# A two-layer transformer block on one core: the last low part of each group of seven products made by ScalarE and an accumulating DMA instead of VectorE

## The chip, the cores and the metric

The kernel runs on one core of one Trainium2 chip. The metric is the device time of one launch in microseconds (us), the median of several runs; lower is better. The core's engines have their own queues and run side by side: TensorE (PE in the profile; PEld is its weight load), VectorE (DVE), ScalarE (ACT), GpSimd (POOL) and SyncE (SP). PE, DVE and ACT compute; SP only issues DMAs here, and POOL issues DMAs and does some elementwise work.

## The reference, cut to what matters

Two layers of the same block are applied to 528 tokens of width 1024 (16 meta tokens and 512 inputs), all in fp32:

```python
def hybrid_layer(x, norm_g, w_in, ...):
    h = rms_norm(x, norm_g)
    q, k, v, gate_a, u_b, gate_b, q_idx, k_idx, w_idx, merge = split(h @ w_in)
    ...                                   # norms and rotary embedding on q, k, q_idx, k_idx
    attn = indexer_sparse_attention(...)  # scores by an indexer, the best 128 keys, softmax, values
    y_a = (attn * silu(gate_a)) @ w_a
    pooled = multiscale_pool(u_b, ...)
    y_b = (pooled * silu(gate_b)) @ w_b
    g_a, g_b = split(sigmoid(merge))
    return x + (g_a * y_a + g_b * y_b) @ w_out
```

What the change touches is how the products with `gate_a` and `merge` (512 + 2048 columns of `w_in`) and with half of `w_out` are computed, in both layers.

## The kernel before

**Split operands.** Each fp32 operand X of a large matmul is held as two tiles of the PE's faster fp32r format: a high part, X rounded, and a low part, X minus that rounded copy. A product is then three matmuls: high by high, high by low, low by high. For weights, ScalarE makes the high part (a copy that rounds) and, in most places, VectorE the low part (a subtraction). For some chunks of weights (`by_dma`) the low part is made another way: ScalarE writes the negated rounded copy, and a DMA that adds (`accum_op=OP.add`, issued by POOL) puts the fp32 weights on top of it, `minus` in L222 to L226.

**Chunks.** Weights come from memory in chunks of 1024 by 256, two raw tiles each, loaded by SP (`w_fetch`), with room for two chunks (four raw tiles). A raw tile is overwritten by the load of the chunk after next once its last reader is done. High and low parts go to a ring of eight `w` tiles of 128 partitions by 1024 elements.

**Groups of seven products.** The chunks in `mixed` (twelve per layer, 24 in all: ten for `gate_a` and `merge`, two for `w_out`) are multiplied by the Strassen-Winograd scheme: weights and activations are cut into 2 by 2 blocks, and seven block products take the place of eight. Each needs a block or a sum of blocks of the weights, called `a12`, `a11`, `s2`, `s1`, `s3`, `s4`, `a22` in the code, each with a high and a low part in one `w` tile. `group_of_products` (L1068) issues the products in the order a11, a12, s2, s1, s3, s4, a22. A product is twelve matmuls: for each of four slices of the depth, (high, high), (high, low), (low, high), weights first. So the low part of a block is first needed by the third matmul of its product. All products of a group add up in three PSUM banks; ScalarE copies partial sums out after a11 (`p1`), s2 (`u2`) and s1 (`p5`), and a product that adds on top of a bank must wait for the copy of it.

**Order of the work.** The preparation of a chunk is a list of nine items, i0 to i8 (`mixed_prep`, L262). Items are taken from a queue as the products go: by the end of product d of a group, at least items up to 5 + 9d/7 of that group have been issued (`LEAD` is 5). So i6 is issued after the second product, i7 after the third and i8 after the fourth. The program order is the queue order for PE and DVE (`manual_schedule`). For ACT, POOL and SP a scheduler orders the instructions when the kernel is built, with an own estimate of times; `marked()` keeps an ACT instruction behind the latest copy out of PSUM that was noted in `mark[0]`, here the copy `p1` for i6 and `u2` for i7.

The items that matter here: i5 makes the high part of s3; i6 the low part of s3, the high part of s4, and issues `first_sum(c + 1)` (L260, an accumulating DMA that adds two blocks of the next chunk); i7 makes the low part of s4 and the high part of a22; i8 the low part of a22, after which the raw tiles are free and `w_load` issues the load of the chunk after next. i1 issues the DMA of L289, which adds s2 onto a12 to give s4.

Between the products, the steps of attention (transposes, logits, values) are issued to PE as filling (`pump`), and the steps that pick the best keys on DVE (MAX8 and MATCH_REPLACE8) are issued as long as a running balance `spare` of estimated PE time minus estimated DVE time is positive (`group_done`, L379). A low part counts 0.60 us in it (`dve_cost`).

Of the kernel before, what the change touches and what calls it, by code (L numbers as in the profile page):

```python
# [10 lines left out]
AF = mybir.ActivationFunctionType  # L11
OP = mybir.AluOpType
# [79 lines left out]
def tile_block(ctx: ExitStack, tc: tile.TileContext, x, meta, w_in, pool_w, w_a, w_b, w_out, rows, hgain, c_tab, out):  # L92
    nc = tc.nc
    act, gp = nc.scalar, nc.gpsimd
# [8 lines left out]
    def f(ap):  # L103
        return ap.bitcast(F32)
# [54 lines left out]
    def w_load():  # L159
        if W["load"] < len(chunks):  # L160
            c = w_place()
            for s in range(2):
                w_fetch(c, s)
# [10 lines left out]
    def w_tile():  # L174
        return wpool.tile([128, 1024], F32R, tag="w", name="w", bufs=8)

    def w_prep_enqueue(casts_first=False, after=None):
# [9 lines left out]
        if c in mixed:  # L187
            prep_q.extend(mixed_prep(c))
            return
# [64 lines left out]
    def marked():  # L254

        return tc.issue_after(mark[0]) if mark[0] else nullcontext()

    def first_sum(c):
        if c in mixed:
            gp.dma_start(raws[c][0][:, 1], raws[c][0][:, 0], accum_op=OP.add)  # L260

    def mixed_prep(c):  # L262

        r0, r1 = raws[c]
        blk = {"a11": r0[:, 0], "a21": r0[:, 1], "a12": r1[:, 0], "a22": r1[:, 1]}
        src = {"a11": "a11", "a12": "a12", "a22": "a22", "s3": "a21", "s2": "s2", "s1": "a11", "s4": "a12"}
        ops = ready[c]
        soon = c <= len(chunks) - 2

        def hi(n):  # L270
            t = w_tile().rearrange("p (s k e) -> p s k e", s=2, k=4)
            ops[n] = t
            with marked():
                act.copy(t[:, 0], blk[src[n]])  # L274

        def lo(n):
            dve.tensor_sub(ops[n][:, 1], blk[src[n]], f(ops[n][:, 0]))

        def i0():
            hi("a12")  # L280
            if soon:
                hi("a11")

        def i1():
            lo("a12")
            blk["s2"] = tmp.tile([128, 544], F32, tag="L", name="s2", bufs=LB)[:, :512].rearrange(
                "p (k e) -> p k e", k=4)
            dve.tensor_add(blk["s2"], blk["a21"], blk["a22"])
            gp.dma_start(blk["a12"], blk["s2"], accum_op=OP.add)  # L289
            (lo if soon else hi)("a11")  # L290

        def i2():
            if not soon:
                lo("a11")
            dve.tensor_sub(blk["a11"], blk["s2"], blk["a11"])

        def i3():
            hi("s2")

        def i4():  # L300
            lo("s2")
            hi("s1")

        def i5():
            lo("s1")
            hi("s3")

        def i6():
            lo("s3")
            hi("s4")  # L310
            first_sum(c + 1)

        def i7():
            lo("s4")
            hi("a22")

        def i8():
            lo("a22")
            del raws[c]
            w_load()  # L320

        def counted(fn):
            def item():
                fn()
                progress[c] += 1
            return item

        progress[c] = 0
        return [counted(fn) for fn in (i0, i1, i2, i3, i4, i5, i6, i7, i8)]

    def flush_prep():
# [1377 lines left out]
```

## Time and profile before

| | |
|---|---|
| median of 3 runs | 728.59 us (727.71 to 729.0) |
| profiled execution | span 726.5 us from the first to the last instruction; no other time of it is given |
| instructions | 16015 |
| DVE busy | 613.6 us (84%) |
| ACT busy | 505.0 us (70%) |
| POOL busy | 256.2 us (35%) |
| mean granted TensorE clock | 0.999 |

The 24 groups lie in four stretches of the span: ten from 167 to 304 us and two from 345 to 367 us (first layer), ten from 521 to 655 us and two from 698 to 720 us (second layer). From one group to the next pass 10.9 to 19.5 us, the longer ones with much filling.

How to read it: a row of the grouped views gives the line, engine, operation, output and inputs, shapes, count, then the busy time in us and the mean of one in ns, then the idle time of the engine just before them and what ended it. All PE and DVE instructions have line 63 (the helper that counts their time); they are told apart by their tiles. `w<-raw,w` on DVE is a low part, `w<-raw` on ACT at L274 a high part, `d<-...` on PE a product into a bank. A row of the timeline gives the start, the duration and how many instructions were merged. PE's busy share says little by itself, since matmuls overlap.

### The profile page before, as it was taken

To read this page: it belongs to the slowest core of one execution; us is meant where nothing else is said; L and a number is where in the kernel's file an instruction comes from. 1 tells how busy PE (TensorE), PEld (TensorE's weight loads), DVE (VectorE), ACT (ScalarE), POOL (GpSimd) and SP (SyncE) were. 2 spreads that over 40 slices of the span, in tenths; PEclk is the share of its full clock that TensorE was granted. 3 is DMA by queue.
4 is the path that set the end of the run, shared out by engine and by line. 5 is a ranking of instruction groups with operands and counts; after the bars stand their busy time and mean duration, and the time that the engine had idled before them with its cause. 6 is when DMAs were issued, how large, how long until landed. Compare 5 with 4: busy or idle time off the path is not lost.

```text
span 726.5 us, 16015 instructions
## 1 busy us (share of the span) xinstructions
PE 720.1 (99%) x5829; PEld 693.9 (96%) x5829; DVE 613.6 (84%) x1546; ACT 505.0 (70%) x1162; POOL 256.2 (35%) x347
## 2 busy tenths in 40 slices
PE   9999999999999999999999999999999999999998
PEld 8999998899999999999999989998899999999997
DVE  5887999998998875888968779999989987768774
ACT  7679735686788887656545796367789888875643
POOL 3751174631222211062447411867041231106200
PEclk9999999999999999999999999999999999999999
DMA  8767765874564434677551788677464554448932
GB/s 268 236 162 176 169 150 117 220 162 100 127 136 117 97 79 117 175 225 182 147 165 59 182 186 197 162 168 164 105 160 103 135 127 93 113 114 268 199 93 73
DMA packets 107406, 109.49 MB, mean 151 GB/s; under 512 B 5888, under 2 KB 86448, under 8 KB 107328
## 3 DMA queue, kind: packets, MB, share of 16 engines
q1 hardware_dynamic: 94576, 74.84, 34.3%
q0 software_dynamic: 12672, 33.56, 25.9%
q8 instruction: 46, 0.75, 0.4%
q14 instruction: 32, 0.26, 0.1%
q10 hardware_dynamic: 80, 0.08, 0.0%
HBM read 66.35 MB, written 8.55 MB: 103 GB/s over the span
## 4 chain that ended last, share of the span: by engine, by line
PE 83%; DVE 7%; DMA 4%; ACT 2%; issue 2%; POOL 1%; SPq 0%; DVEq 0%; ACTq 0%; POOLq 0%
PE d L63 67%; PE a L63 11%; PE v L63 4%; DVE w L63 2%; DMA wo<-raw 1%; DMA w<-raw 1%; DMA xt<-in_x_dram 1%; DMA kept<-res 1%; DMA res<-kept 1%; DVE lt L63 1%; DVE sc L63 1%; POOL hlo L1527 1%; DVE c L63 0%; DVE zb L63 0%; DMA raw<-in_w_out_dram 0%
## 5 line engine op out<-in xcount | busy, mean ns | idle before, releaser
L63 PE MATMUL d<-hhi,w 128*128 128x256 f32 (+3 forms) x1248 | 252.9, 292 | 0.4 <-DVE c L63 0.3
L63 PEld LDWEIGHTS d<-hhi,w 128*128 128x128 f32 x1248 | 200.1, 188 | 4.2 <-DVE c L63 0.7
L63 PE MATMUL d<-hlo,w 128*128 128x256 f32 (+3 forms) x624 | 172.6, 289 | 0.0
L63 DVE TENSOR_TENSOR w<-raw,w 128x512 fp32r<-128x512 f32 (+1 forms) x160 | 119.6, 755 | 13.3 <-ACT w L274 13.1
L63 PEld LDWEIGHTS d<-hlo,w 128*128 128x128 f32 x624 | 117.8, 189 | 1.4 <-issue 0.2
L63 PE MATMUL d<-hsum,w 128*128 128x264 f32 (+1 forms) x720 | 95.1, 285 | 0.0
L274 ACT CAST w<-raw 128x512 fp32r<-128x512 f32 x144 | 86.0, 623 | 9.2 <-DMA raw<-s 4.7
L63 PEld LDWEIGHTS d<-hsum,w 128*128 128x128 f32 x720 | 89.7, 188 | 1.0 <-issue 0.5
L63 PE MATMUL d<-w,hhi 128*128 128x256 f32 x576 | 85.9, 287 | 0.0
L63 PEld LDWEIGHTS d<-w,hhi 128*128 128x128 f32 x576 | 74.7, 188 | 4.5 <-issue 2.7
L260 POOL DMA_DIRECT2D raw<-raw x24 | 21.6, 899 | 131.0 <-DMA raw<-in_w_in_dram 21.1
L63 DVE MATCH_REPLACE8 sc<-m,sc 128x400 f32<-128x400 f32 (+2 forms) x100 | 54.4, 548 | 0.0
L63 DVE MAX8 m<-sc 128x8 f32<-128x400 f32 (+2 forms) x100 | 53.4, 557 | 0.9
L226 POOL DMA_DIRECT2D w<-raw x36 | 32.6, 929 | 61.1 <-ACT w L225 44.5
L289 POOL DMA_DIRECT2D raw<-s x24 | 21.2, 885 | 77.7 <-DVE s L63 28.1
L852 ACT ACTIVATE lt<-lt,mn,NR 128x144 f32<-128x144 f32 (+3 forms) x64 | 42.2, 662 | 8.2 <-DVE mn L63 8.0
L63 PE MATMUL d<-mhi,w 128*128 128x272 f32 (+2 forms) x192 | 45.7, 325 | 0.2 <-ACT sq L701 0.2
L63 PE MATMUL d<-w,hlo 128*128 128x256 f32 x288 | 45.6, 281 | 0.0
L867 POOL TENSOR_SCALAR pm<-lt,rs 128x16 f32<-128x16 f32 x48 | 27.9, 604 | 45.8 <-DVE rs L63 42.0
L773 ACT ACTIVATE r<-a,wab 128x272 f32<-128x272 f32 (+2 forms) x80 | 35.4, 489 | 8.2 <-PE a L63 7.9
L225 ACT ACTIVATE w<-raw 128x1024 fp32r<-128x1024 f32 x36 | 37.5, 1057 | 4.3 <-PE d L63 4.3
L1527 POOL TENSOR_TENSOR hlo<-ta,hhi 128x256 fp32r<-128x256 f32 (+1 forms) x28 | 24.9, 898 | 40.5 <-PE d L63 28.9
(270 smaller groups left out, 1642.1 us busy)
## 6 DMA issues: line engine op xcount, KB each, us to landing
raw<-in_w_in_dram SPq DMA_DIRECT2D x88, 256.0 KB, 3.3
w<-raw POOLq DMA_DIRECT2D x36, 512.0 KB, 5.9
raw<-in_w_in_dram SPq DMA_DIRECT2D x32, 512.0 KB, 4.4
raw<-raw POOLq DMA_DIRECT2D x24, 256.0 KB, 4.0
raw<-s POOLq DMA_DIRECT2D x24, 256.0 KB, 3.3
kept<-res SPq DMA_DIRECT2D x16, 264.0 KB, 3.5
res<-kept SPq DMA_DIRECT2D x16, 264.0 KB, 5.5
raw<-in_w_branch_b_dram SPq DMA_DIRECT2D x8, 512.0 KB, 4.6
```

The costliest lines, as they stand in the source:

```text
L63: return fn(*a, **k)
L225: act.activation(t, raws[c][s], AF.Copy, scale=-1.0)
L226: gp.dma_start(t, raws[c][s], accum_op=OP.add)
L260: gp.dma_start(raws[c][0][:, 1], raws[c][0][:, 0], accum_op=OP.add)
L274: act.copy(t[:, 0], blk[src[n]])
L289: gp.dma_start(blk["a12"], blk["s2"], accum_op=OP.add)
L773: act.activation(r[:, n - 1::-1] if i == 0 else r[:, o:o + e], ps[:, :e], AF.Relu, scale=wab[:, i, h:h + 1])
L852: act.activation(L[hh][:, :n], L[hh][:, :n], AF.Exp, scale=NR[:, i, h:h + 1], bias=mn[:, hh:hh + 1], accum_out=sm[:, hh:hh + 1])
L867: (gp if j < 3 else dve).tensor_scalar(pms[i][:, 2 * j + hh, :], L[hh][:, 0:16], rs[:, hh:hh + 1], None, op0=OP.mult)
L1527: pool_end = gp.tensor_sub(hlo[:, j, a:a + n], d, f(hhi[:, j, a:a + n]))
```

## The change

In i6 the high part of a22 is made right after that of s4, and its low part follows at once by a new helper: ScalarE writes the negated rounded copy into the low half of the tile, and a DMA issued by POOL adds the fp32 block. The low part of a22 on DVE (in i8) is gone; `first_sum(c + 1)` moves from i6 to i7. Nothing else differs. This happens in each of the 24 groups.

```diff
+        def far_lo(n):
+            with marked():
+                act.activation(ops[n][:, 1], blk[src[n]], AF.Copy, scale=-1.0)
+            gp.dma_start(ops[n][:, 1], blk[src[n]], accum_op=OP.add)
...
         def i6():
             lo("s3")
             hi("s4")
-            first_sum(c + 1)
+            hi("a22")
+            far_lo("a22")
 
         def i7():
             lo("s4")
-            hi("a22")
+            first_sum(c + 1)
 
         def i8():
-            lo("a22")
             del raws[c]
             w_load()
```

## The prediction, made before the change was run

> **What bounds the kernel now.** I read the page first (busy shares, the chain that ended last), then PE's waits, then four stretches that hold the 24 groups of seven products, then single groups in the timeline.
>
> ```profile
> span 726.5 us, 16015 instructions
> PE 720.1 (99%) x5829; PEld 693.9 (96%) x5829; DVE 613.6 (84%) x1546; ACT 505.0 (70%) x1162; POOL 256.2 (35%) x347
> PE 83%; DVE 7%; DMA 4%; ACT 2%; issue 2%; POOL 1%; SPq 0%; DVEq 0%; ACTq 0%; POOLq 0%
> ```
>
> PE is never idle for long: 726.5 - 720.1 = 6.4 us in the whole span. Busy time can hide small stalls, because matmuls overlap; so the waits of the weight load (PEld) are the better witness. All of those that name DVE's low parts, DVE's sums or ACT's copies out of PSUM:
>
> ```profile
> PEld d L63 <- ACT p L1095: 1.0, 2, 0.7
> PEld d L63 <- DVE w L63: 1.0, 4, 0.3
> PEld d L63 <- DVE c L63: 0.7, 2, 0.5
> ```
>
> (us in total, times, longest.) That is 2.7 us in all, 0.37% of the span. The four stretches, with columns PE, PEld, DVE, ACT and POOL busy, clock, DMA share and GB/s:
>
> ```profile
> 165.00:305.00 140.00, 139.67 (x1212) 136.37 (x1211) 117.28 (x317) 112.31 (x273) 27.71 (x41) 1.00 0.48 114
> 343.00:368.00 25.00, 24.43 (x196) 23.82 (x195) 23.54 (x37) 13.72 (x29) 11.79 (x15) 1.00 0.64 168
> 520.00:655.00 135.00, 134.68 (x1197) 131.97 (x1196) 113.32 (x308) 111.36 (x268) 28.73 (x41) 1.00 0.50 117
> 696.00:722.00 26.00, 25.81 (x216) 25.36 (x216) 17.47 (x37) 12.60 (x31) 0.86 (x1) 1.00 0.24 61
> ```
>
> In the ten-group stretches DVE (84%) and ACT (80 to 82%) are nearly equally full, and PE has no idle time to speak of. So the change moves work between two engines that both lie beside PE. It can pay only by ending waits of PE, and cost only by making new ones.
>
> **The change, part by part.**
>
> *DVE loses 24 low parts.*
>
> ```profile
> L63 DVE TENSOR_TENSOR w<-raw,w 128x512 fp32r<-128x512 f32 x144 | 99.3, 696 | 13.3 <-ACT w L274 13.1
> L274 ACT CAST w<-raw 128x512 fp32r<-128x512 f32 x144 | 86.0, 623 | 9.2 <-DMA raw<-s 4.7 <-DVE raw L63 2.9 <-DMA raw<-in_w_out_dram 1.1
> L225 ACT ACTIVATE w<-raw 128x1024 fp32r<-128x1024 f32 x36 | 37.5, 1057 | 4.3 <-PE d L63 4.3
> L230 ACT CAST w<-raw 128x1024 fp32r<-128x1024 f32 x36 | 37.3, 1051 | 0.0
> ```
>
> 24 x 0.696 = 16.7 us of DVE. None of it lies on PE's path except where PE waited for DVE. Moreover the pacing in `group_done` counts 0.60 us for a low part and gives what is not used to the selection steps: while these last, the freed time is filled at once. The gain is therefore between 0 and the 2.7 us above. The waits for other low parts and for the sums that stand behind them in DVE's queue can end in part; I take 0.8, about half of the two DVE rows (1.7).
>
> *ACT gains 24 negated copies.* A scaled copy of 1024 elements costs what a cast costs (1057 against 1051 ns), so one of 512 costs what the cast of 512 does, 0.62 us: 24 x 0.62 = 14.9 us. In the ten-group stretches ACT goes from 112.3 to 118.5 of 140 us, 85%. Queued behind the two copies that now come after `hi("s4")` are `u2` and `p5`; the product that adds onto the same bank waits for each. The waits in between take up part of the shift (below, 0.71 us in the second group). Bounds for what PE loses: 0, and 1.0 (the two late copies of the ACT row above, once more). I take 0.4, nearer to 0, since 22 of 24 groups have no such wait now.
>
> *POOL gains 24 accumulating DMAs of 256 KB.*
>
> ```profile
> L260 POOL DMA_DIRECT2D raw<-raw x24 | 21.6, 899 | 131.0 <-DMA raw<-in_w_in_dram 21.1 <-DVE mn L63 19.9 <-DMA raw<-in_w_out_dram 19.3
> L289 POOL DMA_DIRECT2D raw<-s x24 | 21.2, 885 | 77.7 <-DVE s L63 28.1 <-issue 15.3 <-DVE c L63 13.4
> DMA to landing us min/median/max: 3.2/3.3/4.6
> DMA to landing us min/median/max: 3.3/4.0/5.3
> ```
>
> The last two rows are L289's and L260's: from the start of the issue to the landing. Both are DMAs of the new one's kind and size, 0.9 us of POOL each; 24 x 0.9 = 21.6 us on an engine 35% busy. L289 mostly runs alone; L260 starts while loads of raw tiles are in flight. The new one starts then too (below), so I take 4.0, with 3.2 and 5.3 as ends.
>
> The Trainium skill, page DMA: Bandwidth & Descriptors, section Anatomy of one DMA, gives about 2.0 us plus the bytes over 436 GB/s for a DMA issued by GpSimd. That would be 2.6 us for 256 KB, an estimate by that page; no row here goes below 3.2, so the measurement decides, and by the page alone no group below would be late.
>
> *The critical term: does a22's low part arrive in time?* Now it takes 0.69 us of DVE behind the high part. Then it takes a second ACT copy, a POOL issue and a landing. In the second group (rows of ACT, DVE, PE, POOL and SP's queue):
>
> ```profile
> 180.93 1.15 ACT L274 CAST w<-raw 128x512 fp32r<-128x512 f32 x2
> 182.79 0.69 ACT L866 ACTIVATE lt<-lt,rs 128x128 f32<-128x128 f32 x2 [0.71 <-DVE rs L63]
> 183.97 0.61 ACT L274 CAST w<-raw 128x512 fp32r<-128x512 f32 x1
> 184.61 0.69 DVE L63 TENSOR_TENSOR w<-raw,w 128x512 fp32r<-128x512 f32 x1
> 187.70 0.41 PE L63 MATMUL d<-hhi,w 128*128 128x264 f32 x2
> 182.86 0.91 POOL L867 TENSOR_SCALAR pm<-lt,rs 128x16 f32<-128x16 f32 x2 [3.81 <-DVE rs L63]
> 182.31 3.94 SPq L154 DMA_DIRECT2D raw<-in_w_in_dram  x4
> ```
>
> The first row holds the high parts of s3 and s4 and ends at 182.08; the high part of a22 now waits for `u2` and starts at 183.97. It will be free to follow s4's, since its mark is now `p1`. Two copies back to back take 1.15, so a further one adds 0.53: the negated copy ends at 182.08 + 2 x 0.53 = 183.14, and the low part lands at 187.14. PE needs it at 187.70, the third matmul of the product. Slack 0.56 us, without the small POOL work at 182.86, which can come first. The same in the first and the last group, and in two others:
>
> ```profile
> 168.65 1.66 ACT L274 CAST w<-raw 128x512 fp32r<-128x512 f32 x3
> 176.59 0.40 PE L63 MATMUL d<-hhi,w 128*128 128x264 f32 x2
> 349.35 1.14 ACT L274 CAST w<-raw 128x512 fp32r<-128x512 f32 x2 [0.86 <-DMA raw<-s]
> 354.79 1.64 PE L63 MATMUL d<-osum,w 128*128 128x264 f32 x12
> 598.82 1.15 ACT L274 CAST w<-raw 128x512 fp32r<-128x512 f32 x2
> 609.30 0.40 PE L63 MATMUL d<-hhi,w 128*128 128x256 f32 x2
> 711.17 1.16 ACT L274 CAST w<-raw 128x512 fp32r<-128x512 f32 x2
> 718.07 1.21 PE L63 MATMUL d<-osum,w 128*128 128x256 f32 x8
> ```
>
> First group (168.65): 170.31 + 1.06 + 4.0 = 175.37 against 176.59, slack 1.2. The eleventh (349.35; this row already holds a22's high part, so one copy is added): 355.02 against 354.79 + 0.24, the third matmul: slack 0.0. The nineteenth (598.82), with much filling between its products: 605.03 against 609.30, slack 4.3. The last: 717.39 against 718.31, slack 0.9. Read so in all 24 groups, ten have 2.6 us or more, and fourteen between -0.2 and 1.25. Adding up what is late over the 24: 0 at a landing of 3.3, 0.2 us at 4.0, 2.4 us at 4.6, 9.6 us at 5.3. I take 1.0, a little above the median's value.
>
> *What else moves.* The loads that refill the second raw tile wait for the last reader of a22: in the group above the second pair of the SP row went out as DVE's low part ended (184.61 + 0.69); now it goes at the landing, about 2 us later.
>
> ```profile
> 196.31 1.15 ACT L274 CAST w<-raw 128x512 fp32r<-128x512 f32 x2
> ```
>
> Its first reader is this row, 9 us further on, so it costs nothing; were the cover gone, 2 us per group would be the price. `first_sum` moves one item back and behind the new DMA on POOL; it waits for its raw tile's load anyway and is needed by DVE a group later: nothing. Behind the new DMA's wait on POOL stand also the small sums of L867 and L289's DMA; the latter comes near the group's end, after it.
>
> The sum: -0.8 (waits of PE ended) + 0.4 (late copies out) + 1.0 (late low parts) = +0.6 us. Span 726.5 + 0.6 = 727.1. The median of the runs, 728.59, lies 2.1 above the span; so 729.2 us. About 0.2%, 1.5 us, is what a measurement of this kernel can tell from no change; I forecast no such difference.
>
> **The rivals.**
>
> *Faster: DVE was the hidden limit.* Then PE's waits for DVE and for copies queued behind it end all, and nothing is late: -2.7, 725.9 us. For it: DVE is 94% busy in the stretch 343 to 368 (23.54 of 25). Against: the ten-group stretches show less than 0.4 us of PE idle time each. The Trainium skill, Perfetto Trace Analysis, section Optimizing Scalar/DVE Operations, says that with a saturated DVE moving work to Scalar may pay. DVE is at 84%, and PE does not wait for it; the trace bears this out little. Chance 0.22.
>
> *Slower: the low part of a22 is late.* One mechanism, at one place: PE, in order, stops at the third matmul of the seventh product. It decides from a landing of about 4.5 us on, or from the 0.9 us of L867 in front of the issue. At 4.6 the tight groups lose 2.4 us together: with +0.4 and -0.8 as above, +2.0, 730.6 us. At 5.3 it is 9.6 + 0.4 - 0.8 = +9.2, 737.8. For it: L260, with loads beside it, was seen up to 5.3, and the SP row shows loads leaving within 1 us of the new issue. Against: the scheduler may put a22's copies ahead of s4's, which itself waits for a DMA (0.86 in the eleventh group). Chance 0.33.
>
> *It does not relieve DVE:* the selection steps take the freed time in the early groups of each layer. This lowers the gain to about 0.4 and gives 729.6; it belongs to my forecast.
>
> **How the numbers follow.** My forecast, within 1.5 us of before, has 0.45; its own range is 727.2 to 730.0. Faster 0.22, slower 0.33. For 8 in 10 the range reaches down to 726.6, leaving out the end of the faster case, and up to 733.0: at a landing of 4.9 the same slacks lose 4.8 us, and 4.8 + 0.4 - 0.8 = +4.4. About 0.08 and 0.11 are left out.
>
> **What would show it.** Right: DVE's `w<-raw,w` at 512 elements x120, ACT with 24 more copies of 0.62, PE's busy time as before and a22's low part landing 0 to 1 us before the third matmul in about half of the groups. Wrong towards slower: PEld waits for a DMA `w<-raw`, more than 2 us in total, in the groups with little filling. Wrong towards faster: the three PEld rows above gone, with no new one. What I have least hold on is ACT's order, which the scheduler makes anew: if the negated copy is put behind `u2`, every tight group is late by about a product, and I am wrong by 10 us or more.

## The result, and the profile after

| | before | after |
|---|---|---|
| median of four runs in the comparison | 728.36 us (727.71 to 729.0) | 735.83 us (733.54 to 736.28) |
| ratio after / before, 95% interval | | 1.0092 (1.008 to 1.0104) |
| profiled execution, span | 726.5 us | 733.8 us |
| mean granted TensorE clock in it | 0.999 | 0.997 |

The change makes the kernel slower by 7.5 us, 0.9%. The forecast was 729.2 us and no measurable difference; the result lies above the forecast's range (726.6 to 733.0).

The page of the kernel after, span and busy time, against the two rows shown of before:

```profile
span 733.8 us, 16104 instructions
PE 722.4 (98%) x5829; PEld 695.6 (95%) x5829; DVE 597.7 (81%) x1522; ACT 517.5 (71%) x1186; POOL 274.9 (37%) x371
```

DVE did lose its work (613.6 to 597.7 us), ACT and POOL took it over. PE has the same 5829 matmuls, but is without work for 733.8 - 722.4 = 11.4 us instead of 6.4. The groups by line and shape say that the moved work has the size that was expected:

```profile
L63 DVE TENSOR_TENSOR w<-raw,w 128x512 fp32r<-128x512 f32 x120 | 82.0, 689 | 8.4 <-ACT w L274 8.0
L281 ACT ACTIVATE w<-raw 128x512 fp32r<-128x512 f32 x24 | 15.1, 629 | 0.0
L282 POOL DMA_DIRECT2D w<-raw x24 | 21.7, 904 | 104.7 <-ACT w L281 62.3 <-ACT u L1100 42.4
```

So the loss isn't in what the new instructions cost. The waits of the weight load (total us, times, longest) show what PE waits for now:

```profile
PEld d L63 <- DMA w<-raw: 3.5, 3, 2.9
PEld d L63 <- ACT u L1100: 3.1, 3, 1.4
PEld d L63 <- DVE w L63: 1.6, 2, 1.3
```

The first two rows are new. `DMA w<-raw` is the low part of a22 landing late; `ACT u` is the copy `u2` out of a PSUM bank coming late, so that the product s3, which adds onto that bank, must stand. Of the rows of before (ACT `p` 1.0, DVE `w` 1.0, DVE `c` 0.7) the first is gone and the last down to 0.2; DVE `w` is 0.6 higher. The four stretches, in the same columns as for before:

```profile
165.00:305.00 140.00, 139.36 (x1208) 135.82 (x1207) 111.05 (x307) 116.53 (x282) 34.25 (x51) 1.00 0.58 125
343.00:368.00 25.00, 21.24 (x159) 20.82 (x158) 18.26 (x31) 13.07 (x27) 11.29 (x13) 0.93 0.69 170
520.00:655.00 135.00, 133.19 (x1161) 129.34 (x1159) 107.97 (x302) 114.37 (x276) 40.22 (x53) 1.00 0.60 130
696.00:722.00 26.00, 25.61 (x216) 25.19 (x215) 18.96 (x41) 14.68 (x34) 4.30 (x5) 1.00 0.50 122
```

The second one, with the two `w_out` groups of the first layer, stands out: PE has 21.24 us of 25 (24.43 before), and the granted clock is 0.93 there, 1.00 elsewhere. (The stretches are fixed times of a trace that is later and later, so the last three don't hold quite the same work.)

Where the time went can be read by comparing the start of each product in the two traces. The difference grows only at a few places:

| place | us |
|---|---|
| ahead of the first group | +0.3 |
| third group, s3 waits for `u2` (0.8), and little losses behind it | +1.05 |
| fourth to tenth group | -0.1 |
| eleventh group: `p1` no longer waited for (-0.7), low part of s2 late (+1.2), low part of a22 late (+2.9), other (-0.2) | +3.2 |
| twelfth group: matmuls at a lowered clock | +1.3 |
| fourteenth group, s3 waits for `u2` | +1.4 |
| fifteenth group, s3 waits for `u2` (0.9), less 0.3 | +0.6 |
| seventeenth group | -0.4 |
| **sum** | **+7.35** |

The chain through `u2` in three groups takes 3.05 us of it, the eleventh group with what follows from it 4.5 us. The other groups lose nothing to speak of.

**The fourteenth group: a transfer makes ACT late, and ACT makes PE late.** Rows of the timeline (start, duration) of ACT, SP's queue, POOL and PE, first before, at the point where s4 is made and `u2` is copied, then after:

```profile
535.27 0.70 ACT L866 ACTIVATE lt<-lt,rs 128x128 f32<-128x128 f32 x2
535.87 0.61 ACT L274 CAST w<-raw 128x512 fp32r<-128x512 f32 x1
536.90 0.37 ACT L1095 COPY u<-d 128x256 f32<-128x256 f32 x1 [0.42 <-PE d L63]
527.92 0.92 SPq L154 DMA_DIRECT2D raw<-in_w_in_dram  x2
531.80 0.86 POOL L289 DMA_DIRECT2D raw<-s  x1
538.25 1.67 PE L63 MATMUL d<-hsum,w 128*128 128x256 f32 x12
DMA to landing us min/median/max: 3.4/3.4/3.4
```

```profile
541.03 0.70 ACT L871 ACTIVATE lt<-lt,rs 128x128 f32<-128x128 f32 x2
543.34 1.14 ACT L274 CAST w<-raw 128x512 fp32r<-128x512 f32 x2 [1.61 <-DMA raw<-s]
544.38 0.63 ACT L281 ACTIVATE w<-raw 128x512 fp32r<-128x512 f32 x1
544.91 0.35 ACT L1100 COPY u<-d 128x256 f32<-128x256 f32 x1
536.30 1.93 SPq L154 DMA_DIRECT2D raw<-in_w_in_dram  x2
537.57 0.94 POOL L294 DMA_DIRECT2D raw<-s  x1
543.81 0.38 PE L63 MATMUL a<-consts,lt 128*128 128x128 f32 x2
545.32 1.46 PE L63 MATMUL d<-hsum,w 128*128 128x256 f32 x10 [1.13 <-ACT u L1100]
DMA to landing us min/median/max: 5.7/5.7/5.7
```

The last row of each is the landing time of the `raw<-s` DMA above it, which adds s2 onto a12 and so makes s4 (L289 before, L294 after). Read it step by step:

1. Before, the loads that refill the second raw tile went out 3.9 us ahead of that DMA (527.92 and 531.80). After, their last reader is the new accumulating DMA, not DVE, so they go out 1.3 us ahead of it (536.30 and 537.57). Two loads and the addition, of 256 KB each, now run beside each other, and the addition takes 5.7 us to land instead of 3.4.
2. It lands at 537.57 + 5.7 = 543.3. ACT, whose next instruction is the cast of s4, stands for 1.61 us; before it didn't wait there at all.
3. Behind that cast ACT now has two more copies, the high part of a22 and the negated copy, some 0.53 us each, and only then `u2`, at 544.91 to 545.26.
4. PE ended its filling at 544.19 and stands until 545.32, 1.13 us.

Either part alone would have been covered here, or nearly, by an estimate from these rows. Without the two added copies `u2` would end at about 543.34 + 0.61 + 0.35 = 544.3, 0.1 us late; without the late landing ACT would go on at 541.73 and `u2` would be ready before 544.19. ACT's order has a share in this: in the thirteenth group the scheduler put four short instructions of the attention, about 1 us, between a22's high part and its negated copy, so that the new DMA and with it the loads left that much later.

The third and the fifteenth group read the same way. The loads go out 0.9 and 1.1 us ahead of s4's DMA (3.2 and 3.7 before), it lands in 5.1 us in both (3.9 and 4.1 before), and ACT stands for 1.83 and 1.31 us (0.55 in both before). That the waits for `raw<-s` grew in general is seen in ACT's waits, before and after:

```profile
ACT w L274 <- DMA raw<-s: 4.7, 8, 1.0
```

```profile
ACT w L274 <- DMA raw<-s: 11.0, 11, 2.2
```

**The eleventh group: the low part of a22 lands 6.9 us after its issue.** Rows of POOL, SP's queue and PE of the kernel after, and the landing of the new DMA:

```profile
352.35 0.87 POOL L282 DMA_DIRECT2D w<-raw  x1 [2.76 <-ACT w L281]
352.40 7.39 SPq L157 DMA_DIRECT2D raw<-in_w_in_dram  x2
356.24 0.40 PE L63 MATMUL d<-osum,w 128*128 128x264 f32 x2
359.33 1.50 PE L63 MATMUL d<-osum,w 128*128 128x264 f32 x10 [2.69 <-DMA w<-raw]
DMA to landing us min/median/max: 6.9/6.9/6.9
```

A load leaves 0.05 us after the new DMA was issued (the SP row merges it with one 7 us later). PE does two matmuls of the product a22 and stops at the third, the first that needs the low part, for 2.69 us. Earlier in the same group PE stopped in the same way for s2's low part (`w<-s,w`), which stood on DVE behind two slow sums `osum`:

```profile
349.80 0.68 DVE L63 TENSOR_TENSOR w<-s,w 128x512 fp32r<-128x512 f32 x1
350.54 4.41 PE L63 MATMUL d<-osum,w 128*128 128x264 f32 x34 [1.07 <-DVE w L63]
```

What follows the longer stop is seen in windows of the same kernel (columns as above, the clock third from the end; the last window lies inside the second):

```profile
356.00:360.50 4.50, 1.81 (x15) 1.60 (x14) 3.71 (x6) 2.09 (x4) 2.70 (x3) 1.00 0.69 125
360.50:364.50 4.00, 4.00 (x22) 4.00 (x21) 1.84 (x4) 1.56 (x4) 1.28 (x2) 0.57 0.88 268
364.50:368.00 3.50, 3.50 (x31) 3.50 (x30) 1.95 (x4) 2.50 (x5) 0.86 (x1) 1.00 0.57 148
360.90:364.20 3.30, 3.30 (x17) 3.30 (x16) 1.60 (x3) 1.26 (x4) 1.21 (x1) 0.50 0.92 298
```

From 360.9 to 364.2 the granted clock is 0.50 (0.57 in the mean of the 4 us from 360.5 on), and the matmuls start every 0.22 us instead of every 0.12. So the pause costs 2.7 us and then 1.3 more.

### The profile page after: what moved, and what is told of

Same layout as the page of the kernel before. It is cut to its first block, busy times and chain, and to the rows that moved or that the text cites. A ratio compares the mean times of both kernels' runs of the same rounds, so it can differ in the third digit from the quotient of the medians.

```text
span 733.8 us, 16104 instructions
## 1 busy us (share of the span) xinstructions
PE 722.4 (98%) x5829; PEld 695.6 (95%) x5829; DVE 597.7 (81%) x1522; ACT 517.5 (71%) x1186; POOL 274.9 (37%) x371
## 4 chain that ended last, share of the span: by engine, by line
PE 76%; DMA 9%; DVE 6%; issue 3%; ACT 3%; SPq 1%; POOL 1%; POOLq 0%; DVEq 0%; ACTq 0%
PE d L63 61%; PE a L63 11%; PE v L63 4%; DMA raw<-s 3%; DMA w<-raw 2%; DMA xt<-in_x_dram 2%; DVE ta L63 1%; DVE t L63 1%; DMA raw<-in_w_out_dram 1%; DMA wo<-raw 1%; POOL hlo L1532 1%; DVE osum L63 0%; SPq L157 0%; DVE m L63 0%; DVE sc L63 0%
## 5 line engine op out<-in xcount | busy, mean ns | idle before, releaser
L63 DVE TENSOR_TENSOR w<-raw,w 128x512 fp32r<-128x512 f32 (+1 forms) x136 | 102.4, 759 | 8.4 <-ACT w L274 8.0
L274 ACT CAST w<-raw 128x512 fp32r<-128x512 f32 x144 | 84.3, 622 | 13.2 <-DMA raw<-s 11.0
L282 POOL DMA_DIRECT2D w<-raw x24 | 21.7, 904 | 104.7 <-ACT w L281 62.3
L226 POOL DMA_DIRECT2D w<-raw x36 | 33.0, 939 | 61.2 <-ACT w L225 33.0
L260 POOL DMA_DIRECT2D raw<-raw x24 | 21.4, 890 | 73.8 <-DMA raw<-in_w_in_dram 18.7
L294 POOL DMA_DIRECT2D raw<-s x24 | 21.7, 905 | 52.7 <-DVE s L63 19.8
L63 PEld LDWEIGHTS d<-w,hlo 128*128 128x128 f32 x288 | 38.8, 188 | 0.0
```

The costliest lines, as they stand in the source:

```text
L63: return fn(*a, **k)
L226: gp.dma_start(t, raws[c][s], accum_op=OP.add)
L282: gp.dma_start(ops[n][:, 1], blk[src[n]], accum_op=OP.add)
```

## The experiments

Each ran beside the kernel before, on the same chip as it; a ratio stands to the runs of before there (medians 728.26 to 728.55). The theory: the loads of the second raw tile go out later and delay s4's DMA; this and the added copies, which stand ahead of `u2` on ACT, act together; and in the eleventh group the new DMA meets a load. The rivals: ACT's added copies are enough by themselves; the DMA's traffic is enough by itself; the late low part of a22 in the `w_out` groups explains it all.

### One part at a time, and both without the new low part

`act_alone` is the kernel before with ACT's new order; DVE still makes the low part, over the negated copy.

```diff
         def i6():
             lo("s3")
             hi("s4")
-            first_sum(c + 1)
+            hi("a22")
+            with marked():
+                act.activation(ops["a22"][:, 1], blk["a22"], AF.Copy, scale=-1.0)
         def i7():
             lo("s4")
-            hi("a22")
+            first_sum(c + 1)
```

> Only ScalarE's part: the high part of a22 and the negated copy stand behind that of s4 as in the changed kernel, but VectorE then writes the low part over the negated copy, and there is no new DMA. Theory A (chain of both parts: the DMA holds back the refill loads, these slow the DMA that s4 waits for, ACT stands at s4's copy, and the two copies then stand ahead of u2): s4's copy waits as in the kernel before, u2 is later but mostly within its slack, ratio 1.000 to 1.0015. Rival B (two more copies ahead of u2 are enough): the three waits for u2 stay, ratio 1.004 or more.

`dma_alone` is the kernel before with one accumulating DMA of 64 KB per group, which reads a22's raw block where the new DMA does, and adds it onto a tile that nobody uses:

```diff
             hi("s4")
+            with marked():
+                act.copy(dummy[:, 0:1], f(ops["s4"][:, 0, 0, 0:1]))
+            gp.dma_start(dummy, blk["a22"][:, 0, :], accum_op=OP.add)
             first_sum(c + 1)
```

> Only the DMA's part, in a small form: an accumulating DMA of 64 KB that reads the block a22 after s4's high part and writes to a tile that nobody reads; it holds the raw tile about 3 us longer. VectorE makes the low part as before, and the high part of a22 stays behind u2. Theory A: the refill loads go out 2 to 3 us later, the median landing of s4's DMA rises from 3.3 to near 3.7, ACT waits for it nearer to 11 than to 4.7 us, but only s4's own copy stands ahead of u2: ratio 1.000 to 1.002. Rival C (the DMA traffic alone costs it): 1.004 or more. Rival B: 1.000, and no longer waits.

(The small copy on ACT only keeps the DMA behind s4's cast; the tile `dummy` is made ahead.) This DMA moves a quarter of the bytes of the new one, and it isn't behind a22's two copies.

`both_parts` has the two edits together, the small DMA behind the negated copy, and still DVE's low part, so that PE never needs the DMA's result.

> Both suspects together, but with VectorE still making the low part: a22's high part and the negated copy stand ahead of u2 (as in the run with ScalarE's part alone, ratio 1.0005), and a DMA of 64 KB holds the raw tile for about 3 us more (as in the run with the DMA's part alone, 1.0015). Nothing on PE waits for the new DMA itself. Theory A (the two act on each other through the wait for s4's DMA): clearly more than the sum of 1.0020, near 1.004, with waits for u2 of 2 to 3 us as in the run without the w_out groups (1.0042). Rival (the parts only add up): 1.0015 to 1.0025.

Measured: `act_alone` 729.12 us, ratio 1.0005 (0.9996 to 1.0014); `dma_alone` 729.77, 1.0015 (1.0006 to 1.0023); `both_parts` 732.34, 1.0058 (1.0045 to 1.0072). PEld's wait for `u2` and ACT's wait for s4's DMA, in this order of kernels (`dma_alone` has no wait for `u2`):

```profile
PEld d L63 <- ACT u L1097: 1.5, 2, 0.9
```

```profile
ACT w L274 <- DMA raw<-s: 5.0, 6, 2.0
```

```profile
ACT w L276 <- DMA raw<-s: 9.2, 10, 1.9
```

```profile
PEld d L63 <- ACT u L1101: 2.7, 4, 1.2
```

```profile
ACT w L276 <- DMA raw<-s: 8.3, 10, 1.5
```

The copies alone leave the wait for s4's DMA as it was (5.0 against 4.7) and cost nothing that can be measured. They do bring 1.5 us of waits for `u2` in the profiled execution, in the eleventh and the fifteenth group, where s4's DMA landed in 4.8 us with no late load ahead of it; PE's waits for ACT's copies `p` fall from 1.0 to 0.2 us in exchange. The DMA alone, which holds the raw tile and so the loads, doubles ACT's wait (9.2) but PE hardly notices. Together they cost 0.58%, nearly three times the sum of the two (0.20%), and more than the sum's own uncertainty can explain. That is the interaction; near 1.004 was expected. Its longest waits are where the chain puts them: in the fourteenth and the twelfth group s4's DMA landed in 5.4 and 5.3 us, and PE stood for `u2` for 1.2 and 1.0 us.

ACT's copies alone are thus not enough. For the DMA the answer is weaker, since the two edits are not independent. In `both_parts` the copies also put the DMA back: in the fourteenth group the loads leave 1.6 us ahead of s4's DMA, in `dma_alone` 3.3. A DMA as late as the change's without ACT's copies was not run; by the rows of the fourteenth group above `u2` would then be 0.1 us late, an estimate. That the bytes of the new DMA alone don't cost the 0.92% is shown by `a22_first` below, which moves all of them.

### Which groups

`not_out` makes the change in the twenty groups of `gate_a` and `merge` only, `out_only` in the four of `w_out` only; the others keep the items of before.

```diff
+        far = c % (len(chunks) // 2) < len(chunks) // 2 - 2    # >= in out_only
         def i6():
             lo("s3")
             hi("s4")
-            hi("a22")
-            far_lo("a22")
+            if far:
+                hi("a22")
+                far_lo("a22")
+            else:
+                first_sum(c + 1)
```

(with i7 and i8 of before where `far` is false)

> The change in the 20 groups for gate_a and merge only; the four groups for w_out keep the DVE low part. In the changed kernel the stretch of the first two w_out groups is where 4.5 us of the 7.3 us are lost (a low part 2.9 us late, a DVE low part late before it, and a halved clock after it). If these are losses of that stretch itself: about 731.0 us, ratio 1.0035, with the three waits for the copy u2 (0.8, 1.4, 0.9 us) still there. If they are only knock-on effects of being late earlier: ratio stays near 1.009.

> The change in the four w_out groups only. If losses add up by place: 1.0092 less 1.0042, ratio 1.005, with a low part 2 to 3 us late in the eleventh group and a granted clock near half for 3 to 4 us after it. If that lateness came from the shift of 1.2 us that the earlier groups had built up (a chance meeting with the 512 KB load): ratio 1.000 to 1.002, and no dip of the clock.

Measured: `not_out` 731.75 us, 1.0042 (1.0028 to 1.0055), with this wait and no lowered clock:

```profile
PEld d L63 <- ACT u L1106: 2.5, 3, 1.2
```

`out_only` 729.88, 1.0027 (1.0016 to 1.0039), with this wait of PEld:

```profile
PEld d L63 <- DMA w<-raw: 2.1, 2, 1.3
```

So both places count, and neither is the whole. For `out_only` either 1.005 or 1.000 to 1.002 was expected; the ratio lies between them. The sum, 0.69%, is less than the 0.92% of the change. In `out_only` the eleventh group's new DMA left beside a load as well (351.41 and 351.28) but landed in 5.1 us, not 6.9; PE lost 1.3 us there, and the clock stayed at 1.0 behind it in the profiled execution. Two of its twelve runs, with a mean granted clock of 0.997 and 0.998, took 732.4 and 733.1 us, the ten others 728.3 to 731.0. The kernel after shows the same: its one run at a clock of 1.000 took 733.54, still above the forecast's range, the three at 0.997 and 0.998 took 735.5 to 736.3. So the lowered clock goes with some 2 to 3 us of a run, and the change gets into it more often than `out_only`.

### Other orders of the same work

`s4_behind` takes the change and puts s4 behind a22: its high part in i7, its low part in i8.

```diff
         def i6():
             lo("s3")
-            hi("s4")
             hi("a22")
             far_lo("a22")
         def i7():
-            lo("s4")
+            hi("s4")
             first_sum(c + 1)
         def i8():
+            lo("s4")
```

> The change, with s4's high part moved one item back (its mark is then u2) and its low part one more. Theory A: ACT no longer stands ahead of u2 for s4's DMA, so PE's waits for u2 are gone, although the two copies of a22 still stand ahead of u2: at least 3 us faster than the changed kernel, ratio 1.004 to 1.005, the w_out groups' loss remaining; if the low part also lands earlier in the eleventh group, down to 1.000. Rival B: the waits for u2 stay, ratio 1.008 or more.

Measured: 731.15 us, 1.0033 (1.0021 to 1.0045). The waits for `u2` are gone, and so is ACT's wait for s4's DMA: with ACT not standing at s4's cast ahead of `u2`, the chain is cut. The ratio is a little below the 1.004 to 1.005 expected. Another wait has come, mostly since s4's low part is now too late:

```profile
PEld d L63 <- DVE w L63: 4.3, 9, 0.8
```

`a22_first` only swaps two lines of the change: a22's copies and its DMA come ahead of s4's cast.

```diff
             lo("s3")
-            hi("s4")
             hi("a22")
             far_lo("a22")
+            hi("s4")
```

> The change, with a22's two copies issued ahead of s4's copy instead of behind it. Theory A: ACT does them in the time in which it would stand waiting for s4's DMA, and the low part lands 0.5 to 2 us earlier; the refill loads go out earlier too. Waits for u2 below 1.5 us, ratio 1.002 to 1.006, the upper part if the eleventh group is still late. Rival B (two more copies ahead of u2 cost it wherever they stand): 1.007 to 1.010.

Measured: 729.16 us, 1.0014 (1.0005 to 1.0022): of the change's 0.92%, 0.14 is left, less than the 1.002 to 1.006 expected, with all 24 new DMAs and their bytes in place. The copies of a22 now run in the time in which ACT stood for s4's DMA, as in the third group:

```profile
191.40 1.14 ACT L274 CAST w<-raw 128x512 fp32r<-128x512 f32 x2
192.44 0.63 ACT L281 ACTIVATE w<-raw 128x512 fp32r<-128x512 f32 x1
193.14 0.62 ACT L274 CAST w<-raw 128x512 fp32r<-128x512 f32 x1
```

The last row is s4's cast, which no longer stands in front of the others. What is left is mostly one kind of wait of PEld, for the low part of a22:

```profile
PEld d L63 <- DMA w<-raw: 1.7, 3, 0.6
```

The wait for `u2` is 0.4 us in all. In the eleventh group the new DMA left at 349.01, 1.5 us ahead of the load (350.50), and landed in 3.6 us.

`a22_before_s3` goes one step further and puts a22's copies and DMA into i5, ahead of s3's cast.

```diff
         def i5():
             lo("s1")
+            hi("a22")
+            far_lo("a22")
             hi("s3")
         def i6():
             lo("s3")
             hi("s4")
-            hi("a22")
-            far_lo("a22")
```

> The change in all 24 groups, with a22's two copies one place further ahead, before s3's copy. With s4's copy behind them the ratio was 1.0014, PE's waits for a22's DMA 1.7 us. Theory A: the DMA is issued about 0.5 us earlier and these waits end; s3's copy is 1.1 us later, with slack or not: ratio 0.998 to 1.001. If the copies ahead of s3 make its low part late: waits of PE for DVE's low parts above 2 us, ratio 1.002 to 1.004.

Measured: 730.82 us, 1.003 (1.0018 to 1.0042). No low part of a22 is late any more, but `p1` is in the eleventh group (1.2 us; 0.7 before), `p5` in the fourteenth (0.4), and the low part of a11 for the next group in the twelfth and the fifteenth (0.5 each):

```profile
PEld d L63 <- ACT p L1100: 1.6, 2, 1.2
PEld d L63 <- DVE w L63: 1.5, 4, 0.5
```

Both expectations missed: the ratio is above 1.001, yet s3's low part isn't late, and the waits for DVE stay below 2 us.

### The load held back in the eleventh group

`out_load_held` is `out_only` with one more DMA of 64 KB behind the new one, which reads the first raw tile and so keeps the load that met it from going out:

```diff
                 far_lo("a22")
+                with marked():
+                    act.copy(dummy[:, 0:1], f(ops["a22"][:, 0, 0, 0:1]))
+                gp.dma_start(dummy, blk["a21"][:, 0, :], accum_op=OP.add)
```

> The change in the four w_out groups only (ratio 1.0027), with a small accumulating DMA (64 KB) from the block that s3 is made of, issued behind the one for a22: it keeps the first raw tile busy, so that the 512 KB load into it can't leave at the same moment as a22's DMA. If that load is what made a22's DMA land late in the eleventh group (5.1 us there, 6.9 in the changed kernel): it lands in 3.3 to 4.0 us, PE's waits for it fall from 2.1 us to below 1 us, ratio 1.000 to 1.0015. If the lateness has another cause (POOL, the DMA's own path): landing above 4.5, ratio near 1.003.

Measured: 731.38 us, 1.0038 (1.0025 to 1.0052). The new DMA of the eleventh group (issued at 351.17) now lands in 3.35 us, and PE's wait for it there is gone: that it was late because of the load is shown, by one profiled execution of each kernel. The total, however, is worse than that of `out_only`, and outside the 1.000 to 1.0015 expected. Rows of SP's queue, POOL and ACT show why:

```profile
354.70 0.92 SPq L157 DMA_DIRECT2D raw<-in_w_in_dram  x2
355.81 0.88 POOL L297 DMA_DIRECT2D raw<-s  x1
361.59 1.14 ACT L277 CAST w<-raw 128x512 fp32r<-128x512 f32 x2 [1.99 <-DMA raw<-s]
```

and in PEld's waits:

```profile
PEld d L63 <- ACT u L1111: 2.4, 2, 1.5
```

The held loads go out 1.1 us ahead of the next group's s4 DMA, which lands after 5.8 us; ACT stands for 1.99 us, and `u2` is late by 1.5. It is the chain of the fourteenth group, at a place where it wasn't before. The other wait for `u2`, 0.9 us, is in the eleventh group itself: s4's DMA landed in 4.8 us there without a late load ahead of it, as in `act_alone`.

### The best version

`not_out_a22_first` has the change in the twenty groups only, in the order of `a22_first`.

> The same order, a22's copies ahead of s4's, in the 20 groups for gate_a and merge only, and VectorE's low part in the four w_out groups. Theory A: what is left are the late copies u2 in part: ratio 1.000 to 1.002, against 1.0042 with s4's copy first. Rival B: 1.004. If the freed VectorE time is worth something on PE's path, below 1.000.

Measured: 728.54 us, 1.0003 (0.9994 to 1.0011). This doesn't beat the kernel before. With 20 low parts less on DVE, the three waits of PE that the prediction started from fall from 2.7 to 1.8 us, and 1.6 us of new ones come (`u2` 1.1, a22's low part 0.5); the time moves by nothing that can be measured.

## Why the prediction was wrong

**What was right.** DVE has 120 low parts of 512 elements left, 82.0 us of work instead of 99.3; the negated copy takes 0.629 us (0.62 forecast) and POOL's issue 0.904 (0.9); the new DMA's median landing is 3.7 us (4.0 taken). That DVE's time is off PE's path was right too, and the gain of 0.8 us was about right in size: the three waits of before fall from 2.7 to 1.8 us in `not_out_a22_first`. That is partly luck, since most of it is ACT's `p` (1.0 to 0.4) and the 0.8 was taken from DVE's two rows. In the kernel after they come to 1.8 as well, though 1.3 of that is the late low part of s2, a new wait.

**The step that failed is "What else moves".** It said that the loads of the second raw tile go out about 2 us later, which they do, and that this "costs nothing", since their first reader comes 9 us later. It looked for those who wait for the load, and not for those who share the DMA engines with it. In the three groups that lose by it, s4's DMA is issued 0.9 to 1.3 us behind the first of the late loads, lands in 5.1 to 5.7 us instead of 3.4 to 4.1, and holds up ACT in order. Over the 24 groups it takes 4.5 us or more in eight, in two before. The trace of before had a sign of it. The working says that L289, this DMA, "mostly runs alone"; but in the sixteenth to the eighteenth group the loads go out 2.0 to 2.3 us ahead of it, and it lands in 4.2 to 4.6 us there. `dma_alone` shows the step by itself (ACT's wait for s4's DMA 9.2 us instead of 4.7), `out_load_held` makes it in another group.

**The term of the late copies out was mis-sized for that reason:** +0.4 forecast, 3.1 us measured in three groups. It was worked out with s4's cast at the time at which it stood before. ACT's two further copies would then be covered but for 1.5 us, as `act_alone` shows; with s4's cast 0.6 to 1.8 us later, measured against PE's own delay, they aren't.

**The term of the late low parts was mis-sized, too:** +1.0 forecast, spread thinly over fourteen groups; 3.5 us measured, 2.9 of it in the eleventh group. The working gave this group a slack of 0.0, so the place was right. Its DMA was issued 1.3 us later than the working had it (352.35 instead of 349.35 + 1.14 + 0.53 = 351.02), but PE was 1.45 us later there too (356.24 instead of 354.79), so the issue was in time. What failed is the landing: 6.9 us, past the end of 5.3 that was taken from the row of L260, beside a load that left at the same moment. The range's upper end allowed this term 4.8 us, more than it took. What took the result out of the range is the late copies out, which had 0.4 in the sum there too, and the clock, which had nothing.

**Not in the sum at all** was the lowered clock after the pause: 1.3 us in the trace.

**The slower rival** named this stop at the third matmul of the seventh product, and a little over half of the loss is there and in what follows (2.9 and 1.3 us). The rest has another mechanism, which no rival named. Its reason against, that a22's copies might be put ahead of s4's by the scheduler, didn't come about; `a22_first` shows what that order would have brought, a ratio of 1.0014. The step with "least hold", ACT's order, was the right one to doubt, but not in the form given: the negated copy isn't behind `u2`, `u2` is behind the negated copy.

**What stays open.** The parts of the change leave some 0.2% of the loss unexplained by their sum. The trace puts it into the longer landing in the eleventh group (6.9 against 5.1 us) and the clock behind it, but why the pause lowers the clock in three of four runs of the change and in two of twelve of `out_only` was only argued from its length (2.7 against 1.3 us). DVE's low part of s2 came 1.2 us late in the eleventh group, because DVE's sums `osum` stretched there; whether the change is the cause wasn't settled. In the same group s4's DMA lands late without the new DMA as well (4.5 us before, 4.8 in `act_alone`), for a reason that isn't known. A third pair of raw tiles, which might take the loads out of the chain, was not tried.

## What to carry to other kernels

When the last reader of a buffer becomes a DMA, the buffer comes free a landing later, so ask not only who waits for its refill, but which other transfer the refill will now run beside, and which engine, in order, stands behind that one. Price a moved step with its neighbours moved too: two edits that are cheap alone (0.05% and 0.15% here) can use up the same slack, or push each other later, and cost 0.58% together. And freeing an engine that is 84% busy is worth no more than the bound engine's waits for it, here 0.9 us, and new waits use that up: 20 low parts less changed the time by 0.03%, within the uncertainty.

## What the runs showed of the hardware

**The same kind of DMA landed in 3.2 to 6.9 us, the longest beside a load.** 256 KB from SBUF onto SBUF with addition (a22's low part in the kernel after) landed in 3.2 us at best, 3.7 at the median and 6.9 at worst, the last beside a load issued 0.05 us later. With that load held back it was 3.35. The distance to the load isn't all: before, s4's DMA took 4.6 us in the seventeenth group and 3.3 in the twenty-first, both with loads 2.0 us ahead. The Trainium skill, page DMA: Bandwidth & Descriptors, section Issuing engines are not separate DMA queues, says that transfers started by different engines run on the same 16 DMA engines and interleave. The trace agrees: SP issued the loads and POOL the additions, and in the fourteenth group the addition took 3.4 us with the loads 3.9 us ahead of it and 5.7 with them 1.3 us ahead.

**A pause of 2.7 us was followed by a halved clock.** After PE's stop from 356.6 to 359.3 the granted clock was 0.50 from 360.9 to 364.2, and matmuls came every 0.22 us instead of 0.12. The stop of 1.3 us in `out_only` had no such effect in its profiled execution. The Trainium skill, page TensorE: Matmul & The Clock Gate, Part 1, says that the clock falls to half after an idle window of about 3.4 us. Half is what the trace shows, but the pause was shorter than that window; the measurement decides.

**A DVE subtraction of 0.68 us took 3.00 beside POOL's elementwise work.** In the kernel before, `raw<-s,raw` of the eleventh group ran from 343.65 to 346.65, with POOL's sums of squares and a DMA issue at 343.33 to 347.27; after, where it ended as POOL's sums began, it took 0.68 us, and the two `osum` sums that ran beside them 3.20 instead of 0.99. That POOL is the cause wasn't tested. The Trainium skill, page SBUF — State Buffer, section Who interferes with whom, says that a DVE instruction with two inputs in SBUF contends with a GpSimd instruction that reads SBUF; the two durations agree with it.
